# Scans a step behind their sigmoids, low parts behind the scans, and mapped weights kept in SBUF for the first chunk

## The chip, the cores and the metric

The kernel runs on one core of one Trainium2 chip. The metric is the device time of one execution in microseconds.

## What is computed

A two-layer trunk over 2048 tokens of 1024 channels, in f32:

```python
# layer 0: pooling mixer
u, z = split(rms_norm(x, a_norm) @ a_w_in)
pooled = trailing means of u over 2, 4, 8, 16 frames (4 channel groups) - u
x = x + ((pooled @ w_group per group) * a_scale * silu(z)) @ a_w_out
x = x + (p[0] @ ple_w[0]) * sigmoid(x @ ple_gate_w[0])
# keys and values once; layer 1: stick-breaking attention, 16 heads of 64
k, v = split(rms_norm(x, kv_norm) @ w_kv); q, z = split(rms_norm(x, b_norm) @ b_w_in)
A[t,s] = beta[t,s] * prod_{s<j<t} (1 - beta[t,j]),  beta = sigmoid(q.k / 8), s < t
x = x + ((A @ v) * silu(z)) @ b_w_out
x = x + (p[1] @ ple_w[1]) * sigmoid(x @ ple_gate_w[1])
```

Pooling is linear in time and `w_group` acts on channels, so the kernel multiplies `w_in`'s u half by `w_group` once ("mapped weights", `wf`) and pools the mapped product.

## The kernel before

**Tiles.** Tokens go through in four chunks of 512. Channels lie on partitions, and a matmul is 128 x 128 weights by 128 x 512 activations. Each f32 operand is split into a high part, rounded to f32r by ScalarE, and a low part (the difference); a product is three matmuls, high by high, high by low, low by high (L223, L227, L230 in `product`, L244, L246, L249 in `product2`, L490 for q, k and v, where activations are the weights side).

**Weights.** `plan` lists all weight units in the order of use. `pump` loads them ahead into buffers of the tag `wpair`, at most `UNITS` = 9 at a time: a unit that is used again is split once, written to DRAM (L152) and read back ready from there (L145, `wpair<-once` or `wpair<-wf`). `take` hands units out, `give_back` frees them. Raw loads (`wraw`, L148), x tiles and the columns of `w_in` (`uraw`, L262) share four buffers, tag `io`.

**First chunk.** For group g, `fold` makes the mapped weights on PE: 48 matmuls of 256 columns (L279) from the group weights and from four blocks of `w_in`, cast and split by `fold_load` (L266 `uh`, L267 `ul`). ScalarE and VectorE scale the result and split it (L285, L286) into `wf`, a buffer of the tag `at`, of which there are three; SP writes it to DRAM (L289), and `pump` reads it back (L145) as the next units. `pump` stops at the mapped units of `plan` (`src` None) until `fold` has written them. `mixer` runs the groups 3, 2, 1, 0: the fold, the z product (L223 to L230 with weights `wz_a`), then the u product with the mapped weights. `prep(0)` splits x (L119, L120), squares it (L350) and sums the squares with one-column matmuls (L355).

**Attention.** A slot is one head, one chunk of queries and one chunk of keys; it has four steps, of 128 queries each. Step n does, in program order: `turn` of step n-5 (four transposes, L736, of the products into a `psa` bank; ScalarE's high part `at`, L739; VectorE's low part, L740), `front` of step n (two matmuls for the logits, L721 and L722; the sigmoid of the negated logits, L724; a running product along keys, L726, called the scan below), a share of the dense products of the next chunk (`fill`), `gather` of step n-7 (L748 with the high part, L749 with the low), and another share. `psa`, `psl`, `pso`, `psd` have two PSUM banks each; `pp`, which holds sigmoids and running products, has nine buffers.

**Order.** A scheduler puts the instructions of each engine in order at build time by priorities and its own model; program order holds only where a dependency or `keep_in_program_order` demands it, which binds an instruction behind the one traced just before it on its engine. `state["pin"]` does that to the first matmul of each k pair of `product`, in the slots of the last chunk. The dense products of chunk c+1 run in the slots of chunk c, layer 1's output products in the slots of the last.

**z of layer 1.** In `gate_z` the first block of z is made before the norm is known; the norm is then broadcast (`bcast`, L297) at the 20th matmul of the next product, and the two kept tiles are multiplied by it.

Of the kernel before, what the change touches and what calls it, by code (L numbers as in the profile page):

```python
# [15 lines left out]
P = 128  # L16
# [20 lines left out]
def trunk_kernel(ctx, tc, x, p, a_norm, wu_t, wz_a, w_group, a_scale, a_w_out, kv_norm, w_kv,  # L37
# [158 lines left out]
    for s in range(NSUB):  # L196
        for g in (3, 2, 1, 0):
            if s == 0:
                plan_group(g)
            plan_block("za", wz_a, g, g_a, True)  # L200
            plan_block("wf", None, g)
        for b in range(4):
            plan_block("ao", a_w_out, b, order=PAIRS[::-1])
        for b in range(4):
            plan_block("ag", gate_a, b)
            plan_block("al", ple_a, b, order=PAIRS[:1])
        if s + 1 == NSUB:
# [5 lines left out]
        plan_kvq(1)  # L213
    for c in range(NSUB):
        plan_post()

# [53 lines left out]
    def fold(g):  # L270
        parts = maps.pop(g)
        (wg, _), = take(1)
        for kts in PAIRS:
            ps = dense().rearrange("q (e n) -> q e n", e=2)
            for e, kt in enumerate(kts):
                ks = slice(kt % 4 * P, kt % 4 * P + P)
                for c in range(2):
                    for l, r in ((0, 0), (1, 0), (0, 1)):
                        T.matmul(ps[:, e], parts[c, kt // 4][l][:, ks], wg[:, r, c],  # L279
                                 start=(c == 0 and l == r), stop=(c == 1 and r == 1))  # L280
# [8 lines left out]
            nc.sync.dma_start(out=d, in_=f(pr))  # L289
        give_back()  # L290
# [43 lines left out]
    def prep(s):  # L334
        ck = chunk[s]
        ck["x"] = []
        for o in range(KT):
            if s:
                xin = io("xin")
                nc.sync.dma_start(out=xin, in_=x[o * P : (o + 1) * P, s * W5 : (s + 1) * W5])  # L340
            else:
                xin = first_x[o]
            pr = pair("xp")
            split(pr, xin, G if s else V)
            ck["x"].append(pr)
            if s:
                gather_squares(ck, "acc1", o, xin)
            else:
                sq = tmp("sq")
                A.activation(out=sq, in_=xin, func=AF.Square)  # L350
                if o == 0:
                    sums = turned()
                for j in range(4):
                    tc.keep_in_program_order(
                        T.matmul(sums[:, 0, j : j + 1], sq[:, j * P : (j + 1) * P], ones,  # L355
                                 start=(o + j == 0), stop=(o == KT - 1 and j == 3)))
# [224 lines left out]
    def gate_z(s):  # L581
# [133 lines left out]
    def front(st, j):  # L715
# [6 lines left out]
        T.matmul(ps[:, :w], qb[:, qs], kk[:, :w], start=False, stop=True)  # L722
        pp = ppt("pp")
        A.activation(out=pp[:, r0:], in_=ps[:, :w], func=AF.Sigmoid, scale=-1.0)  # L724
        least = floor[:, r0:][:, ::-1] if st["diag"] else floor[:, 0:1].to_broadcast([P, w])
        V.tensor_tensor_scan(out=pp[:, r0:][:, ::-1], data0=pp[:, r0:][:, ::-1], data1=least,  # L726
                             initial=1.0 if st["diag"] else st["carry"][j], op0=ALU.mult, op1=ALU.max)
        st["carry"][j] = pp[:, r0 : r0 + 1]
        st["a"].append((pp, r0))

    def turn(st, kt):
        j0 = kt if st["diag"] else 0
# [4 lines left out]
        at = att("at")  # L737
        cs = slice(j0 * P, W5)
        A.copy(out=at[:, 0, cs], in_=pt[:, cs])  # L739
        V.tensor_tensor(out=at[:, 1, cs], in0=pt[:, cs], in1=f(at[:, 0, cs]), op=ALU.subtract)  # L740
        st["at"][kt] = at

    def gather(st, kt):
        cs = slice((kt if st["diag"] else 0) * P, W5)
# [53 lines left out]
        return (parts * 24.0) / (64 * (c + 1) - (5 if c < NSUB - 1 else 0))  # L798

    nc.scalar.dma_start(out=g_a, in_=a_norm)  # L800
    fold_load(3)
    pump()
    load_first()
    wq["by"] = nc.sync
    for dst, v in ((g_s, a_scale), (g_b, b_norm), (g_kv, kv_norm), (gs[:, 0:1], k_norm), (gs[:, 1:2], b_q_norm)):
        nc.scalar.dma_start(out=dst, in_=v)
    V.scalar_tensor_tensor(out=gqk, in0=gs[:, 1:2], scalar=HD ** -0.5, in1=gs[:, 0:1],
                           op0=ALU.mult, op1=ALU.mult)
    wq["cap"] = UNITS
    for _ in fold(3):  # L810
        pass
    for _ in prep(0):
# [11 lines left out]
    def fill(share):  # L824
        nonlocal owed, count
        owed += share
        while owed >= 1.0:
# [3 lines left out]
            if count % 36 == 0 and kept:  # L831
                keep(*kept.pop(0))

    for n in range(4 * len(slots) + LAG_G):
        i, j = divmod(n, 4)
        x_ = rate(i)
        i2, j2 = divmod(n - LAG_T, 4)
        if 0 <= i2 < len(slots):
            turn(active[i2], j2)
        if i < len(slots):  # L840
            state["pin"] = slots[i][0] == NSUB - 1
            if j == 0 and i + 1 < len(slots):
                begin(i + 1)
            if j == 3 and i + 1 < len(slots):
                begin_v(i + 1)
            front(active[i], j)
        fill(x_ / 2)
        i3, j3 = divmod(n - LAG_G, 4)
        if 0 <= i3 < len(slots):
            gather(active[i3], j3)  # L850
            if j3 == 3:
                active.pop(i3)
        fill(x_ / 2)
# [69 lines left out]
```

## Time and profile before

| | us |
|---|---|
| median of 3 runs | 2830.56 |
| lowest, highest | 2822.56, 2832.28 |
| the profiled execution | 2831.42 |
| its span, first to last instruction | 2829.6 |
| PE busy in it | 2731.6 |
| DVE (VectorE) busy | 1846.1 |
| ACT (ScalarE) busy | 1272.0 |
| POOL (GpSimd) busy | 878.4 |

PE is TensorE's matmuls, PEld its weight loads, which overlap them; SPq is SP's DMA queue. A row of a group has the source line, the engine, output and inputs by their names in the program, the count, the busy time and the mean of one in ns, then the idle time of the engine just before such instructions and what ended most of it. A row of a stretch has from:to, its length, the busy time and instructions of the five, PE's granted clock (1.00 is full), the DMA engines' share and GB/s. A wait's row has the total, the times and the longest.

### The profile page before, as it was taken

What the parts mean: (1) busy time and instruction counts of PE and PEld (TensorE: products, weight loads), DVE (VectorE), ACT (ScalarE), POOL (GpSimd) and SP (SyncE); (2) the same over time, 40 slices, a digit from 0 to 9 for tenths busy, and PEclk for the clock granted to TensorE, in tenths of its full rate; (3) what the DMA queues carried; (4) which work ended last, traced back from release to release, by engine and by line L of the source; (5) the groups of instructions that cost most, each with busy time, mean ns of one, the idle gap of its engine ahead of it and who ended that gap; (6) DMA issues with size and microseconds to landing.
All of it is one profiled execution on the core that took longest, in us unless ns stands there. A gap on an engine that the chain in (4) does not pass through costs nothing.

```text
span 2829.6 us, 38580 instructions
## 1 busy us (share of the span) xinstructions
PE 2731.6 (97%) x13400; PEld 2257.3 (80%) x13400; DVE 1846.1 (65%) x2369; ACT 1272.0 (45%) x2496; POOL 878.4 (31%) x699
## 2 busy tenths in 40 slices
PE   7999989998999999999999999999999999999999
PEld 6778867877878888878888788777877888888767
DVE  4646445757244677755678888756667777778763
ACT  4335444345444345544444555544445444444441
POOL 1255533556533244443222434211211201112002
PEclk8999999999999999999999999999999999999999
DMA  6756899978887855667885447567567767667535
GB/s 231 260 170 235 313 336 367 353 217 275 300 296 272 270 166 175 201 201 249 273 289 179 134 136 229 164 214 241 170 221 236 247 203 260 196 221 243 163 120 186
DMA packets 302799, 651.81 MB, mean 230 GB/s; under 512 B 51462, under 2 KB 84230, under 8 KB 302604
## 3 DMA queue, kind: packets, MB, share of 16 engines
q1 hardware_dynamic: 301020, 648.02, 69.3%
q8 instruction: 106, 1.74, 0.3%
q10 hardware_dynamic: 1584, 1.33, 0.1%
q14 instruction: 89, 0.73, 0.1%
HBM read 479.82 MB, written 161.02 MB: 226 GB/s over the span
## 4 chain that ended last, share of the span: by engine, by line
PE 68%; DVE 4%; DMA 4%; issue 1%; ACT 1%; POOL 1%; SPq 0%; ACTq 0%; DVEq 0%; POOLq 0%
PE psd L490 14%; PE psd L223 9%; PE psd L227 9%; PE psd L230 9%; PE psa L736 7%; PE pso L749 4%; PE pso L748 4%; PE psl L722 4%; PE psl L721 4%; DVE pp L726 2%; PE psd L244 2%; PE psd L249 2%; PE psd L246 2%; DMA wpair<-once 1%; DMA kk<-kd 1%
## 5 line engine op out<-in xcount | busy, mean ns | idle before, releaser
L726 DVE TENSOR_TENSOR_SCAN pp<-pp,floor 128x512 f32<-128x512 f32 (+3 forms) x640 | 769.7, 1220 | 166.5 <-ACT pp L724 164.5
L490 PE MATMUL psd<-wpair,x 128*128 128x512 f32 x2304 | 593.2, 398 | 11.7 <-DMA wpair<-once 3.0
L740 DVE TENSOR_TENSOR at<-psa,at 128x512 fp32r<-128x512 f32 (+3 forms) x640 | 379.1, 599 | 251.4 <-ACT at L739 249.8
L739 ACT CAST at<-psa 128x512 fp32r<-128x512 f32 (+3 forms) x640 | 331.3, 522 | 412.9 <-PE psa L736 388.7
L490 PEld LDWEIGHTS psd<-wpair,x 128*128 128x128 f32 x2304 | 427.5, 190 | 100.5 <-ACT qs L530 4.7
L724 ACT ACTIVATE pp<-psl 128x512 f32<-128x512 f32 (+3 forms) x640 | 330.1, 535 | 262.7 <-PE psl L722 159.8
L736 PE MATMUL psa<-ident,pp 128*128 128x128 f32 x2176 | 349.3, 276 | 29.1 <-DVE at L740 21.9
L736 PEld LDWEIGHTS psa<-ident,pp 128*128 128x128 f32 x2176 | 272.9, 142 | 107.7 <-DVE at L740 37.2
L749 PE MATMUL pso<-at,vv 128*128 128x512 f32 (+3 forms) x640 | 271.7, 425 | 0.4 <-DVE at L740 0.2
L721 PE MATMUL psl<-kk,qa 128*128 128x512 f32 (+3 forms) x640 | 243.8, 382 | 11.3 <-DMA kk<-kd 6.5
L748 PE MATMUL pso<-at,vv 128*128 128x512 f32 (+3 forms) x640 | 236.0, 371 | 3.1 <-ACT at L739 3.1
L223 PE MATMUL psd<-x,wpair 128*128 128x512 f32 x592 | 233.4, 394 | 2.5 <-ACT sg L466 2.5
L722 PE MATMUL psl<-kk,qb 128*128 128x512 f32 (+3 forms) x640 | 235.1, 368 | 0.0
L227 PE MATMUL psd<-x,wpair 128*128 128x512 f32 x592 | 232.6, 393 | 0.0
L230 PE MATMUL psd<-x,wpair 128*128 128x512 f32 x592 | 232.1, 392 | 0.0
L223 PE MATMUL psd<-xp,wpair 128*128 128x512 f32 x512 | 206.2, 403 | 8.8 <-DMA wpair<-wf 5.6
L227 PE MATMUL psd<-xp,wpair 128*128 128x512 f32 x512 | 205.3, 401 | 0.0
L230 PE MATMUL psd<-xp,wpair 128*128 128x512 f32 x512 | 204.3, 400 | 0.0
L133 POOL TENSOR_TENSOR wpair<-wraw,wpair 128x512 fp32r<-128x512 f32 x98 | 146.4, 1500 | 116.9 <-ACT wpair L131 116.7
L721 PEld LDWEIGHTS psl<-kk,qa 128*128 128x128 f32 x640 | 122.1, 191 | 36.0 <-ACT pp L724 12.9
L459 POOL TENSOR_TENSOR xj<-x 128x512 f32<-128x512 f32 x64 | 105.4, 1650 | 141.9 <-DVE sg L470 137.7
L764 POOL TENSOR_TENSOR os<-os,zt 128x512 f32<-128x512 f32 x32 | 46.3, 1446 | 306.3 <-ACT os L763 247.6
(162 smaller groups left out, 4696.8 us busy)
## 6 DMA issues: line engine op xcount, KB each, us to landing
wpair<-once SPq DMA_DIRECT2D x384, 512.0 KB
once<-wpair SPq DMA_DIRECT2D x80, 512.0 KB
kk<-kd SPq DMA_DIRECT2D x320, 128.0 KB
vv<-vd SPq DMA_DIRECT2D x160, 256.0 KB
wpair<-wf SPq DMA_DIRECT2D x64, 512.0 KB
once<-kp SPq DMA_DIRECT2D x36, 512.0 KB
wraw<-in_a_w_out_dram SPq DMA_DIRECT2D x64, 256.0 KB
wraw<-in_gate_a_dram SPq DMA_DIRECT2D x64, 256.0 KB
```

Of the source, the lines that this page charges most:

```text
L223: ins = T.matmul(ps, hi, acts[kt][:, 0], start=(i == 0), stop=False)
L227: T.matmul(ps, hi, acts[kt][:, 1], start=False, stop=False)
L230: T.matmul(ps, lo, acts[kt][:, 0], start=False, stop=(i == n))
L490: T.matmul(ps, ck["x2"][kt][:, xh, tk], u[:, wh, 0], start=(kt == 0 and xh == wh), stop=(kt == KT - 1 and wh == 1))
L721: T.matmul(ps[:, :w], qa[:, qs], kk[:, :w], start=True, stop=False)
L722: T.matmul(ps[:, :w], qb[:, qs], kk[:, :w], start=False, stop=True)
L726: V.tensor_tensor_scan(out=pp[:, r0:][:, ::-1], data0=pp[:, r0:][:, ::-1], data1=least, initial=1.0 if st["diag"] else st["carry"][j], op0 ...
L736: T.transpose(pt[:, j * P : (j + 1) * P], pp[:, r0 + kt * P : r0 + (kt + 1) * P], ident)
L739: A.copy(out=at[:, 0, cs], in_=pt[:, cs])
L740: V.tensor_tensor(out=at[:, 1, cs], in0=pt[:, cs], in1=f(at[:, 0, cs]), op=ALU.subtract)
L748: T.matmul(po[:, cs], vv[:, kt, :], at[:, 0, cs], start=(st["diag"] and kt == 0), stop=False)
L749: T.matmul(po[:, cs], vv[:, kt, :], at[:, 1, cs], start=False, stop=(st["last"] and kt == 3))
```

## The change

1. `fold` writes the mapped weights straight into buffers of the tag `wpair` and appends them to the units held; `pump` doesn't read them back in the first chunk. The write to DRAM stays, for the later chunks.
2. At the start the group weights are loaded before the columns of `w_in`, and the queue of units opens fully right behind x. The squares of chunk 0 and their matmuls come behind all splits.
3. In `gate_z` the broadcast goes to the 9th matmul, and the two kept tiles are multiplied at the 21st of this product and of the next.
4. `front` returns its scan, which is issued a step later, behind the next step's sigmoid; `turn` returns its low part, which is issued behind that scan. Both are bound behind what was traced before them on VectorE.
5. `state["pin"]` holds in the slots of the last two chunks.

```diff
     def pump():
...
-            if src is None and key not in once:
+            if src is None and (key not in once or wq["out"] < first_chunk):
                 return
...
-            pr = att("wf").rearrange("q l (e n) -> q l e n", e=2)
+            pr = pool.tile([P, 2, 2, WB], F32R, tag="wpair", name="wpair", bufs=UNITS)
...
+            assert plan[wq["out"]][0] == ("wf", g, kts) and wq["out"] - wq["back"] < UNITS
+            held.append((pr, kts))
+            wq["out"] += 1
             d = once["wf", g, kts] = scratch(f"wf{g}_{kts[0]}", [P, 2, 2, WB])
             nc.sync.dma_start(out=d, in_=f(pr))
...
-                sq = tmp("sq")
-                A.activation(out=sq, in_=xin, func=AF.Square)
-                if o == 0:
+                if o == KT - 1:
                     sums = turned()
-                for j in range(4):
...
+                    for i in range(KT):
+                        sq = tmp("sq")
+                        A.activation(out=sq, in_=first_x[i], func=AF.Square)
...
-                    if first and o == 2 and i == 20:
-                        ck["rb2"] = rb = bcast(ck["r2"], "y")
-                        for e, zr in enumerate(first):
-                            V.tensor_tensor(out=zr, in0=zr, in1=rb, op=ALU.mult)
-                            put(e, zr)
+                    if first and o == 2 and i == 9:
+                        ck["rb2"] = bcast(ck["r2"], "y")
+                    if first and o in (2, 3) and i == 21:
+                        zr = first[o - 2]
+                        V.tensor_tensor(out=zr, in0=zr, in1=ck["rb2"], op=ALU.mult)
+                        put(o - 2, zr)
...
     nc.scalar.dma_start(out=g_a, in_=a_norm)
+    pump()
     fold_load(3)
-    pump()
     load_first()
     wq["by"] = nc.sync
+    wq["cap"] = UNITS
+    pump()
...
+    scan = None
     for n in range(4 * len(slots) + LAG_G):
...
-            turn(active[i2], j2)
+        low = turn(active[i2], j2) if 0 <= i2 < len(slots) else None
+        due, scan = scan, None
         if i < len(slots):
-            state["pin"] = slots[i][0] == NSUB - 1
+            state["pin"] = slots[i][0] >= NSUB - 2
...
-            front(active[i], j)
+            scan = front(active[i], j)
+        if due:
+            due()
+        if low:
+            low()
         fill(x_ / 2)
```

Lines in the changed kernel: L225, L229, L232 for L223, L227, L230; L268 and L269 for L266 and L267; L281 for L279; L287 and L288 for L285 and L286; L294 for L289; L358 and L361 for L350 and L355; L302 for L297; L728, L729, L731 for L721, L722, L724; L736 for the scan L726; L748, L751, L754 for the turn's L736, L739, L740; L761 and L762 for L748 and L749.

What moves, at three places. First SP's queue in the first chunk, at the mapped weights of group 2 (`wf2_0` is their first unit in DRAM, `once` a split z unit's copy). Before:

```order
L289 DMA wf2_0_804<-wf_799 128x1024
L289 DMA wf2_2_824<-wf_819 128x1024
L289 DMA wf2_4_844<-wf_839 128x1024
L145 DMA wpair_866<-wf2_0_804 128x1024
L145 DMA wpair_868<-wf2_2_824 128x1024
L289 DMA wf2_6_864<-wf_859 128x1024
L145 DMA wpair_870<-wf2_4_844 128x1024
L145 DMA wpair_872<-wf2_6_864 128x1024
L148 DMA wraw_962<-in_wz_a_dram 128x512
L152 DMA once16_923<-wpair_916 128x1024
L262 DMA uraw_975<-in_wu_t_dram 128x512
```

And now:

```order
L294 DMA wf2_0_796<-wpair_791 128x1024
L294 DMA wf2_2_816<-wpair_811 128x1024
L148 DMA wraw_946<-in_wz_a_dram 128x512
L294 DMA wf2_4_836<-wpair_831 128x1024
L294 DMA wf2_6_856<-wpair_851 128x1024
L152 DMA once16_907<-wpair_900 128x1024
L264 DMA uraw_959<-in_wu_t_dram 128x512
```

The four reads are gone, and the next z load and the columns for the next map follow the writes.

Second VectorE in the slots of chunk 2 (a scan has `floor` among its inputs; a low part writes `at`; the rest belongs to dense products). Before:

```order
L726 SCALAR_TENSOR_TENSOR pp_16354<-pp_16354,floor_67 128x256
L726 SCALAR_TENSOR_TENSOR pp_16382<-pp_16382,floor_67 128x384
L740 TENSOR_TENSOR at_16316<-psa_16311,at_16316 128x512
L740 TENSOR_TENSOR at_16348<-psa_16343,at_16348 128x512
L726 SCALAR_TENSOR_TENSOR pp_16429<-pp_16429,floor_67 128x512
L469 TENSOR_TENSOR sg_16880<-psd_16882,sg_16880 128x512
L726 SCALAR_TENSOR_TENSOR pp_16455<-pp_16455,pp_16325,floor_67 128x512
```

And now:

```order
L736 SCALAR_TENSOR_TENSOR pp_16320<-pp_16320,floor_67 128x256
L120 TENSOR_TENSOR ple_16369<-pin_16367,ple_16369 128x512
L736 SCALAR_TENSOR_TENSOR pp_16348<-pp_16348,floor_67 128x384
L754 TENSOR_TENSOR at_16343<-psa_16338,at_16343 128x512
L133 TENSOR_TENSOR wpair_16539<-wraw_16540,wpair_16539 128x512
L754 TENSOR_TENSOR at_16388<-psa_16383,at_16388 128x512
L736 SCALAR_TENSOR_TENSOR pp_16395<-pp_16395,floor_67 128x512
L754 TENSOR_TENSOR at_16413<-psa_16408,at_16413 128x512
```

Scans and low parts stood in pairs, the scans further ahead; now they mostly alternate.

Third ScalarE at the start, ahead of the first z weights (`xp` the split of x, `sq` its squares, `uh` the high part of a block of `w_in`). Before:

```order
L350 ACTIVATE sq_536<-xin_353 128x512
L119 CAST xp_542<-xin_355 128x512
L350 ACTIVATE sq_545<-xin_355 128x512
L119 CAST xp_551<-xin_357 128x512
L119 CAST xp_560<-xin_359 128x512
L137 ACTIVATE wpair_367<-wraw_368,g_a_105 128x256 x2
```

And now:

```order
L119 CAST xp_509<-xin_359 128x512
L358 ACTIVATE sq_513<-xin_345 128x512
L358 ACTIVATE sq_519<-xin_347 128x512
L358 ACTIVATE sq_525<-xin_349 128x512
L358 ACTIVATE sq_531<-xin_351 128x512
L358 ACTIVATE sq_537<-xin_353 128x512
L358 ACTIVATE sq_543<-xin_355 128x512
L268 CAST uh_341<-uraw_327 128x512
L137 ACTIVATE wpair_361<-wraw_362,g_a_105 128x256 x2
```

The squares stand behind the casts, and the last block's cast, which stood ahead of all of this, stands right ahead of the z weights.

More of the change, by code (lines that the diff above doesn't have):

```diff
@@ L348, in prep @@
             else:
-                sq = tmp("sq")
-                A.activation(out=sq, in_=xin, func=AF.Square)
-                if o == 0:
+                if o == KT - 1:
                     sums = turned()
-                for j in range(4):
-                    tc.keep_in_program_order(
-                        T.matmul(sums[:, 0, j : j + 1], sq[:, j * P : (j + 1) * P], ones,
-                                 start=(o + j == 0), stop=(o == KT - 1 and j == 3)))
+                    for i in range(KT):
+                        sq = tmp("sq")
+                        A.activation(out=sq, in_=first_x[i], func=AF.Square)
+                        for j in range(4):
+                            tc.keep_in_program_order(
+                                T.matmul(sums[:, 0, j : j + 1], sq[:, j * P : (j + 1) * P], ones,
+                                         start=(i + j == 0), stop=(i == KT - 1 and j == 3)))
             yield
@@ L724, in front, with scan @@
         A.activation(out=pp[:, r0:], in_=ps[:, :w], func=AF.Sigmoid, scale=-1.0)
[L725 to L729, printed above, removed]
+        def scan():
+            least = floor[:, r0:][:, ::-1] if st["diag"] else floor[:, 0:1].to_broadcast([P, w])
+            tc.keep_in_program_order(
+                V.tensor_tensor_scan(out=pp[:, r0:][:, ::-1], data0=pp[:, r0:][:, ::-1], data1=least,
+                                     initial=1.0 if st["diag"] else st["carry"][j], op0=ALU.mult, op1=ALU.max))
+            st["carry"][j] = pp[:, r0 : r0 + 1]
+            st["a"].append((pp, r0))
+        return scan
     def turn(st, kt):
@@ L739, in turn @@
         A.copy(out=at[:, 0, cs], in_=pt[:, cs])
-        V.tensor_tensor(out=at[:, 1, cs], in0=pt[:, cs], in1=f(at[:, 0, cs]), op=ALU.subtract)
         st["at"][kt] = at
+        return lambda: tc.keep_in_program_order(
+            V.tensor_tensor(out=at[:, 1, cs], in0=pt[:, cs], in1=f(at[:, 0, cs]), op=ALU.subtract))
     def gather(st, kt):
```

4 lines of the change are left out of this document (2 added, 2 removed).

## The prediction

> **What bounds the kernel now.** I read the head of the page first, then the clock, the stretches of time, the waits of PE stretch by stretch, and last SP's queue and the order of the engines.
>
> ```profile
> span 2829.6 us, 38580 instructions
> PE 2731.6 (97%) x13400; PEld 2257.3 (80%) x13400; DVE 1846.1 (65%) x2369; ACT 1272.0 (45%) x2496; POOL 878.4 (31%) x699
> core 0: 2829.6 us, clock 0.984
> ```
>
> PE is the bound: it is idle for 2829.6 - 2731.6 = 98.0 us, and the clock that it was not granted is 1.6% of the span, 45 us, part of that while idle (the whole run took 2831.4 us). The change leaves PE's matmuls as they are, in number and shape; so all that it can win lies in those two sums, and the question is where they lie. Three places matter. The first is the first chunk, columns PE, PEld, DVE, ACT, POOL, then granted clock, DMA share and GB/s:
>
> ```profile
> 79.00:86.00 7.00, 5.70 (x14) 4.48 (x15) 3.73 (x7) 2.44 (x7) 0.87 (x1) 0.51 0.87 295
> 113.00:120.00 7.00, 5.97 (x14) 4.74 (x15) 3.67 (x6) 2.25 (x6) 2.09 (x2) 0.52 0.88 304
> 147.00:151.00 4.00, 3.98 (x11) 3.15 (x12) 0.84 (x1) 1.25 (x3) 4.00 (x4) 0.57 0.82 298
> ```
>
> PE's waits around these three stretches, one answer each:
>
> ```profile
> PE psd L223 <- DMA wpair<-wf: 3.3, 1, 3.3
> ...
> PE psd L223 <- DVE wpair L138: 3.2, 1, 3.2
> ...
> PE psd L223 <- DMA wpair<-wf: 2.3, 1, 2.3
> ```
>
> Each time PE has finished a group's z product and waits for the mapped weights; the clock halves right after. (The second is put down to VectorE, but that instruction works on other units; a read of mapped weights was in flight there too.) SP's queue at the first of them shows why:
>
> ```profile
> 72.08 1.63 SPq L289 DMA_DIRECT2D wf<-wf  x3
> 74.77 1.66 SPq L145 DMA_DIRECT2D wpair<-wf  x2
> 77.10 0.32 SPq L289 DMA_DIRECT2D wf<-wf  x1
> 78.12 5.19 SPq L145 DMA_DIRECT2D wpair<-wf  x2
> 83.38 0.42 SPq L148 DMA_DIRECT2D wraw<-in_wz_a_dram  x1
> ```
>
> And PE's next matmul there:
>
> ```profile
> 80.30 0.77 PE L223 MATMUL psd<-xp,wpair 128*128 128x512 f32 x1 [3.30 <-DMA wpair<-wf]
> ```
>
> The weights lie in SBUF by 72 us, go out to DRAM, and come back behind that write; PE wants them 3.30 us before 80.30, at 77.0 us.
>
> The second place is attention in chunks 2 and 3, where PE stands idle in a few short stretches; the last row but two is the steady rest:
>
> ```profile
> 1540.00:1700.00 160.00, 155.80 (x794) 129.24 (x793) 136.24 (x156) 84.14 (x170) 64.84 (x47) 1.00 0.48 147
> 1770.00:1804.00 34.00, 27.27 (x150) 21.73 (x149) 27.94 (x36) 18.24 (x38) 3.06 (x2) 0.95 0.47 143
> 1854.00:1869.00 15.00, 10.53 (x48) 7.70 (x48) 14.01 (x17) 9.26 (x18) 0.56 (x2) 0.89 1.00 341
> 1917.00:1934.00 17.00, 12.42 (x66) 9.96 (x66) 12.61 (x20) 9.30 (x18) 1.11 (x1) 0.90 1.00 324
> 2057.00:2078.00 21.00, 15.24 (x75) 11.12 (x75) 17.73 (x22) 12.66 (x27) 2.59 (x2) 0.92 0.80 274
> 2129.00:2147.00 18.00, 14.94 (x85) 11.15 (x84) 17.76 (x24) 12.11 (x25) 0.30 (x1) 1.00 0.99 328
> 2147.00:2600.00 453.00, 452.74 (x2321) 376.60 (x2320) 340.29 (x409) 208.06 (x402) 61.55 (x40) 1.00 0.69 222
> 2676.00:2732.00 56.00, 49.00 (x243) 36.36 (x244) 49.22 (x58) 30.98 (x63) 2.54 (x2) 0.94 0.35 113
> 2732.00:2752.00 20.00, 18.32 (x91) 14.01 (x90) 7.66 (x11) 5.96 (x12) 0.45 (x1) 1.00 0.25 80
> ```
>
> Where PE loses, VectorE is busy 74 to 99% of the time; from 2147 to 2600 us, where attention steps and dense products alternate evenly, PE loses 0.3 us in 453.
>
> **The first chunk (mapped weights).** Removed: 16 reads of 512 KB, the waits for them, and SP's standing behind them. The waits are 3.3 + 3.2 + 2.3 = 8.8 us. The half clock after them: 5.70 us of PE work at 0.51 would take 2.9 us at full clock, so 2.8 go; likewise 5.97 x 0.48 = 2.9 and 3.98 x 0.43 = 1.7. Together 8.8 + 7.4 = 16.2 us.
>
> [...]
>
> What is late next: the fourth z load of the next group and the loads for its map, which SP issues from 83.38 us on, behind the reads. With the reads gone SP gets there about 78 us, some 5.5 us earlier, which is as much as PE gains; so they should keep their distance. If they don't, PE waits for the next map instead, and of 5.4 us a group little is left (a rival below). The added wait, a wpair buffer for the map's result, is for a unit used nine units before, thus the same quarter of the group before, whose product PE has finished; the write to DRAM stays, but nothing near reads it. Range of this term: -17 to -4.
>
> **The start.** The first map may begin as soon as its group weights and two of four column blocks are there; before, PE stood until these rows:
>
> ```profile
> 13.26 0.34 ACTq L806 DMA_DIRECT2D gs<-in_b_q_norm_dram  x1
> 14.31 0.58 PE L279 MATMUL psd<-wpair,uh 128*128 128x256 f32 x1 [14.31 <-ACT wpair L131]
> 14.91 0.41 PE L279 MATMUL psd<-wpair,uh 128*128 128x256 f32 x1
> 15.12 0.41 PE L279 MATMUL psd<-wpair,ul 128*128 128x256 f32 x1
> 21.45 3.31 ACT L137 ACTIVATE wpair<-wraw,g_a 128x256 fp32r<-128x256 f32 x8
> 21.65 7.60 PE L355 MATMUL pst<-ones,sq 128*128 128x1 f32 x48
> 33.52 3.41 PE L355 MATMUL pst<-ones,sq 128*128 128x1 f32 x16
> ```
>
> The clock over the last of it:
>
> ```profile
> 24.50:41.60 17.10, 17.10 (x60) 15.10 (x61) 4.43 (x11) 4.47 (x12) 1.23 (x2) 0.50 0.94 345
> ```
>
> PE can start some 6 us earlier, but gains nothing: ScalarE still passes eight casts and six squares, and now the fourth block's cast too (the group weights' cast has left that stretch, so the count is the same), before the z weights at about 21.5 us. The last third of the map, 18 matmuls, waits for that cast; then come the 64 one-column matmuls, whose 7.60 + 3.41 = 11.0 us are in one piece now. Before, PE had the map behind it at 21.65. So PE is later by 18 matmuls, at the 0.21 us between the starts at 14.91 and 15.12 3.8 us, less the idle before 14.31 that no longer counts and less whatever the clock recovers sooner from dense work after 37 us. I take +1.5 us, between -3 (the clock back a window earlier) and +5.
>
> **Attention.** One scan and one low part a step, and no instruction less:
>
> ```profile
> L726 DVE TENSOR_TENSOR_SCAN pp<-pp,floor 128x512 f32<-128x512 f32 (+3 forms) x640 | 769.7, 1220 | 166.5 <-ACT pp L724 164.5
> L736 PE MATMUL psa<-ident,pp 128*128 128x128 f32 x2176 | 349.3, 276 | 29.1 <-DVE at L740 21.9
> L740 DVE TENSOR_TENSOR at<-psa,at 128x512 fp32r<-128x512 f32 (+3 forms) x640 | 379.1, 599 | 251.4 <-ACT at L739 249.8
> ```
>
> VectorE needs 1.22 + 0.60 = 1.82 us a step. PE's own part of a step is shorter: in 1770 to 1804 it did 150 matmuls in 27.27 us busy, 0.18 us each, and a step has eight, 1.45 us. So a bunch of steps with no dense matmul between them is VectorE's, and PE waits. Before, the idle time of the six stretches up to 2147 is 4.2 + 6.7 + 4.5 + 4.6 + 5.8 + 3.1 = 28.9 us, and the clock missing in four of them 0.05 x 34 + 0.11 x 15 + 0.10 x 17 + 0.08 x 21 = 6.7: 35.6 us.
>
> Counted in PE's order, runs of four or more turns without a dense matmul between them: before, from chunk 1's end until products grow short, 17, 4, 8, 8 and 12, which are the last five of the six stretches in order; after, 5, 4, 4, 4, 4, 8, 4, 12 and 4. As many turns, 49 each, but the run of 17 and one of 8 are broken up (the wider pin). At the end, where products have run out, 37 before and 36 after. Two long runs and the run of 4 remain at 3.1 + 4.6 + 1.7 + 4.5 + 1.7 = 15.6; the six new short ones I put at 1.5 each, 9 us, between nothing (the buffers carry four steps) and 3; the thin loss of the first stretch at 2. That is 26.6, 9 us less. Against it stands VectorE's order: before, in 172 of chunk 2's 192 steps a scan stood 7 or 8 steps ahead of the last low part; after, in 145 of them 5, which is the lag that the loop itself gives. Two scans, 2.4 us, are no longer done when a run begins. With half of that at two runs in the middle and half at the end, 3 us. So -6, between -16 and +12. The scan that no longer stands waiting for its sigmoid (164.5 us) is VectorE's gain, and PE sees it only in the runs, where it is in the sum. The bcast moved from the 20th to the 9th matmul lands at the same place in PE's order, 6.8 us of matmuls after its norm, and so costs nothing; the two products behind it are spread over work that VectorE has room for.
>
> **Sum.** -16.2 + 1.5 - 6 = -20.7 against the profiled execution's 2831.4 us, which is 0.9 above the median of 2830.6: **2810 us**.
>
> **The rivals.**
> *The loads take the reads' place.* PE then waits for the next map's columns at each group, as long as before less a microsecond or so, and the clock falls again. For it: SP's queue is in order and those loads are its next rows. Against: they depended on nothing else at 83.38 us. The sum is -3 + 1.5 - 4, about 2825 us.
> *VectorE in lockstep: slower.* Scans and low parts are bound to what stands ahead of them, five steps ahead at most, in all 13 runs; each run pays the 2.4 us of the two scans that were ahead before, nothing of the breaking up is won: -16.2 + 1.5 + 13 x 2.4 = +16.5, 2847 us. It decides from 1.8 us a run on. For it: PE waited on low parts already (21.9 us); against: 1.82 us a step is the same sum of work in either order. [...]
> *The runs are cured.* The low part, no longer behind two or three scans, frees its bank in time, and the short runs cost nothing: -16.2 + 1.5 - 20 = 2796 us. Steady 2147 to 2600 speaks for it, the unchanged run of 12 against.
>
> **How the numbers follow.** Forecast 0.60, loads 0.16, lockstep 0.12, cured 0.12. A measurement of this kernel can tell about 0.3%, 8.5 us, from no change: faster is below 2822, slower above 2839. Of the forecast 0.58 lies below 2822; the cured runs do whole; of the loads 0.03. Faster 0.73. Same takes 0.02 + 0.13 + 0.03 = 0.18, slower the lockstep's 0.09. The range leaves out lockstep and the lower part of the cured case: 2796 to 2828.
>
> **What would show it.** Right: no wait of L225 on mapped weights and a granted clock over 0.95 between 60 and 150 us; the first chunk's end 15 us earlier; the first matmul near 8 us, yet the zs product no earlier; fewer idle stretches between 1700 and 2100. Wrong: waits of PE on L269's columns in the first chunk (loads), or idle before the transposes over 45 us in all (lockstep).

## The result, and the profile after

| | before | after |
|---|---|---|
| median, us (13 runs each) | 2828.37 | 2833.48 |
| lowest, highest | 2821.71, 2832.28 | 2828.38, 2837.83 |
| ratio, 95% interval | | 1.0021 [1.0012, 1.0031] |

The changed kernel is 5 us slower where 20 us less was forecast; by the bound of 0.3% that is no change, and it lies above the range. The head of its page:

```profile
span 2831.7 us, 38727 instructions
PE 2729.6 (96%) x13400; PEld 2250.0 (79%) x13400; DVE 1832.6 (65%) x2369; ACT 1275.0 (45%) x2496; POOL 873.3 (31%) x699
core 0: 2831.7 us, clock 0.986
```

PE's busy time (2731.6 us before, 2729.6 now) and clock (0.984, 0.986) hardly moved, so the same sum of losses must lie elsewhere. The first chunk, columns as before:

```profile
60.00:150.00 90.00, 90.00 (x466) 77.46 (x465) 66.32 (x116) 36.63 (x74) 32.02 (x33) 1.00 0.57 202
```

The matmuls of the first chunk's products wait for no read of mapped weights:

```profile
L225 PE MATMUL psd<-xp,wpair 128*128 128x512 f32 x512 | 203.5, 398 | 0.5 <-DMA wpair<-once 0.5
```

The kernel before, over the same 90 us:

```profile
60.00:150.00 90.00, 81.04 (x390) 68.23 (x391) 56.14 (x108) 34.16 (x69) 25.20 (x27) 0.91 0.73 254
```

That part did what was foreseen: no idle time, full clock. To follow the gain I take the time at which the same piece of PE's work is reached, counting the matmuls of the trace (13400 in each):

| matmul | before, us | after, us | difference |
|---|---|---|---|
| 500th | 127.9 | 115.9 | -12.0 |
| 1000th | 240.3 | 224.2 | -16.1 |
| 2000th | 476.3 | 460.8 | -15.5 |
| 6500th (chunk 2's slots begin) | 1421.2 | 1406.8 | -14.4 |
| 10000th (110 us into chunk 3's) | 2139.2 | 2132.4 | -6.8 |
| 12000th | 2530.3 | 2525.1 | -5.2 |
| 13000th (chunk 3's slots end) | 2734.0 | 2734.3 | +0.3 |

16 us are won in the first 1000 matmuls and given back in the attention of chunks 2 and 3. The groups of attention, of after:

```profile
L736 DVE TENSOR_TENSOR_SCAN pp<-pp,floor 128x512 f32<-128x512 f32 (+3 forms) x640 | 779.0, 1219 | 5.2 <-ACT pp L731 4.6
L754 DVE TENSOR_TENSOR at<-psa,at 128x512 fp32r<-128x512 f32 (+3 forms) x640 | 378.7, 595 | 312.9 <-ACT at L751 311.1
L748 PE MATMUL psa<-ident,pp 128*128 128x128 f32 x2176 | 357.4, 276 | 45.0 <-DVE at L754 23.7 <-DVE pp L736 13.8 <-DVE hl L120 4.6
```

The scan no longer waits for its sigmoid (166.5 us, now 5.2), but VectorE then waits ahead of low parts (251.4, now 312.9), and PE's transposes wait 45.0 us for 29.1. 13.8 of it is new: they wait for the scan itself. One such place, VectorE and then PE of after (start, duration, instruction, idle time before it and who ended it):

```profile
1434.09 1.21 DVE L736 TENSOR_TENSOR_SCAN pp<-pp,floor 128x512 f32<-128x512 f32 x1
1435.22 0.66 DVE L754 TENSOR_TENSOR at<-psa,at 128x512 fp32r<-128x512 f32 x1
1438.11 0.69 DVE L767 TENSOR_TENSOR os<-pso,os 64x512 f32<-64x512 f32 x1 [2.23 <-ACT os L766]
1438.84 1.28 DVE L736 TENSOR_TENSOR_SCAN pp<-pp,floor 128x512 f32<-128x512 f32 x1
```
```profile
1437.53 0.49 PE L761 MATMUL pso<-at,vv 128*128 128x512 f32 x1
1441.45 0.88 PE L748 MATMUL psa<-ident,pp 128*128 128x128 f32 x3 [3.43 <-DVE hl L120]
```

And ScalarE there:

```profile
1434.88 0.63 ACT L731 ACTIVATE pp<-psl 128x512 f32<-128x512 f32 x1
1435.76 0.60 ACT L731 ACTIVATE pp<-psl 128x512 f32<-128x512 f32 x1 [0.25 <-PE psl L729]
```

Sigmoids ended at 1435.51 and 1436.36, and VectorE was idle 2.23 us up to 1438.11, yet no scan ran between 1435.3 and 1438.84: L767, the sum of the two halves of a head's output, stood ahead of it and waited for ScalarE's copy. So the binding does hold scans that could run. PE's 3.43 us, though, ended by its row with L120 and not with a scan: L120 reads keys that stand transposed in one of the two `psa` banks, and the next transposes need a bank. The clock was halved (0.51 granted) from 1440.8 to 1447.7. That is a reading of one place. Whether the binding is the cause, and of the whole loss, the experiments had to show.

### The profile page after: what moved, and what is told of

It reads as the page before. It is cut to its first block, busy times and chain, and to the rows that moved or that the text cites. A ratio compares the mean times of both kernels' runs of the same rounds, so it can differ in the third digit from the quotient of the medians.

```text
span 2831.7 us, 38727 instructions
## 1 busy us (share of the span) xinstructions
PE 2729.6 (96%) x13400; PEld 2250.0 (79%) x13400; DVE 1832.6 (65%) x2369; ACT 1275.0 (45%) x2496; POOL 873.3 (31%) x699
## 4 chain that ended last, share of the span: by engine, by line
PE 78%; DMA 8%; DVE 7%; ACT 2%; issue 2%; POOL 1%; SPq 1%; ACTq 0%; DVEq 0%; POOLq 0%
PE psd L496 15%; PE psd L225 11%; PE psd L229 11%; PE psd L232 11%; PE psa L748 7%; PE pso L762 4%; PE psl L729 4%; PE psl L728 3%; PE pso L761 3%; DVE pp L736 3%; PE psd L251 2%; PE psd L248 2%; PE psd L246 2%; DMA wpair<-once 2%; DVE at L754 1%
## 5 line engine op out<-in xcount | busy, mean ns | idle before, releaser
L736 DVE TENSOR_TENSOR_SCAN pp<-pp,floor 128x512 f32<-128x512 f32 (+3 forms) x640 | 779.0, 1219 | 5.2 <-ACT pp L731 4.6
L496 PE MATMUL psd<-wpair,x 128*128 128x512 f32 x2304 | 582.9, 395 | 10.0 <-ACT wpair L137 3.9
L754 DVE TENSOR_TENSOR at<-psa,at 128x512 fp32r<-128x512 f32 (+3 forms) x640 | 378.7, 595 | 312.9 <-ACT at L751 311.1
L751 ACT CAST at<-psa 128x512 fp32r<-128x512 f32 (+3 forms) x640 | 330.9, 523 | 378.3 <-PE psa L748 358.7
L731 ACT ACTIVATE pp<-psl 128x512 f32<-128x512 f32 (+3 forms) x640 | 333.4, 535 | 305.8 <-PE psl L729 194.8
L748 PE MATMUL psa<-ident,pp 128*128 128x128 f32 x2176 | 357.4, 276 | 45.0 <-DVE at L754 23.7
L748 PEld LDWEIGHTS psa<-ident,pp 128*128 128x128 f32 x2176 | 272.9, 141 | 132.0 <-DVE at L754 38.7
L762 PE MATMUL pso<-at,vv 128*128 128x512 f32 (+3 forms) x640 | 275.1, 430 | 0.6 <-DVE at L754 0.6
L728 PE MATMUL psl<-kk,qa 128*128 128x512 f32 (+3 forms) x640 | 244.3, 382 | 13.2 <-DMA kk<-kd 9.8
L761 PE MATMUL pso<-at,vv 128*128 128x512 f32 (+3 forms) x640 | 238.7, 374 | 7.6 <-DMA once<-kp 5.4
L729 PE MATMUL psl<-kk,qb 128*128 128x512 f32 (+3 forms) x640 | 236.0, 370 | 0.0
L225 PE MATMUL psd<-x,wpair 128*128 128x512 f32 x592 | 233.5, 394 | 0.0
L232 PE MATMUL psd<-x,wpair 128*128 128x512 f32 x592 | 232.5, 393 | 0.0
L229 PE MATMUL psd<-x,wpair 128*128 128x512 f32 x592 | 232.5, 393 | 0.0
L225 PE MATMUL psd<-xp,wpair 128*128 128x512 f32 x512 | 203.5, 398 | 0.5 <-DMA wpair<-once 0.5
L229 PE MATMUL psd<-xp,wpair 128*128 128x512 f32 x512 | 201.7, 394 | 0.0
L232 PE MATMUL psd<-xp,wpair 128*128 128x512 f32 x512 | 201.2, 394 | 0.0
L133 POOL TENSOR_TENSOR wpair<-wraw,wpair 128x512 fp32r<-128x512 f32 x98 | 139.0, 1423 | 153.6 <-ACT wpair L131 152.5
L728 PEld LDWEIGHTS psl<-kk,qa 128*128 128x128 f32 x640 | 122.8, 192 | 40.8 <-ACT pp L731 11.2
L761 PEld LDWEIGHTS pso<-at,vv 128*128 128x128 f32 x640 | 122.0, 191 | 27.7 <-ACT at L751 11.0
```

What stands on the lines that cost most here:

```text
L225: ins = T.matmul(ps, hi, acts[kt][:, 0], start=(i == 0), stop=False)
L229: T.matmul(ps, hi, acts[kt][:, 1], start=False, stop=False)
L232: T.matmul(ps, lo, acts[kt][:, 0], start=False, stop=(i == n))
L496: T.matmul(ps, ck["x2"][kt][:, xh, tk], u[:, wh, 0], start=(kt == 0 and xh == wh), stop=(kt == KT - 1 and wh == 1))
L728: T.matmul(ps[:, :w], qa[:, qs], kk[:, :w], start=True, stop=False)
L748: T.transpose(pt[:, j * P : (j + 1) * P], pp[:, r0 + kt * P : r0 + (kt + 1) * P], ident)
```

## The experiments

**Theory:** the binding of the scan behind everything that was traced before it on VectorE holds ready scans back, and this costs what the first chunk wins. **Rivals:** the wider pin does it; the delay by a step does it (bound or not); the low part's binding does it; the first chunk's gain is itself undone later by its loads; and, as the expectations below have it (theory C), any change gives the scheduler another order of attention, which costs by chance.

**1. Parts alone and left out.** Five kernels, each with some of the parts. All of the change but part 4 (`front` scans at once, `turn` makes its low part at once, neither bound):

```diff
-            scan = front(active[i], j)
+            front(active[i], j)
...
-        if due:
-            due()
-        if low:
-            low()
```

> The whole change without its part 4: scans and low parts are issued as before, in the scheduler's free order; the first chunk's weights, the start, the broadcast and the wider pin stay. Theory V (VectorE's bound order costs what the first chunk saves): the first chunk keeps its 16 us, attention loses nothing: 2812 us, ratio to before 0.994. Theory P (the wider pin costs it): no better than the whole change, 2833 us, 1.002. Theory C (a scheduler that is given other input puts attention in another order, and any change of it costs by chance): anywhere, 2812 to 2840.

2815.7 us, 0.9951 [0.9935, 0.9968]. All but the wider pin:

```diff
-            state["pin"] = slots[i][0] >= NSUB - 2
+            state["pin"] = slots[i][0] == NSUB - 1
```

> The whole change without its part 5: only the last chunk's slots bind the first matmul of each k pair. Theory V: the loss stays, 2830 to 2836 us, 1.001. Theory P: the loss goes, 2812 to 2816 us, 0.995. Theory C: anywhere between.

2821.1 us, 0.9977 [0.9965, 0.9989]. Parts 1 and 2 alone (first chunk and start; of the diff the hunks of `pump`, `fold`, `prep` and the start):

> The kernel before with parts 1 and 2 alone: mapped weights kept in SBUF and the new start. All theories but C: the first chunk's 16 us reach the end, since attention is as before: 2812 us, 0.994. Theory C: the scheduler's order of attention changes with it and takes part of it back: 2815 to 2830.

2819.8 us, 0.9964 [0.9952, 0.9977]. Part 4 alone (scan and low part a step later, bound; the hunks of `front`, `turn` and the loop but for `state["pin"]`):

> The kernel before with part 4 alone: scans a step later, low parts behind them, both bound. Theory V: slower by what the whole change lost in attention, 16 to 20 us: 2844 to 2848 us, 1.006. Theory P: no different from before, 2828 us, 1.000.

2832.9 us, 1.0016 [1.0005, 1.0028]; its profiled execution, span 2819.9 us, was the shortest of its runs. Part 5 alone, the wider pin, against the kernel before:

```diff
-            state["pin"] = slots[i][0] == NSUB - 1
+            state["pin"] = slots[i][0] >= NSUB - 2
```

> The kernel before with part 5 alone, the wider pin. The first four runs left 12 us that the pin costs beside part 4, and 4 us that it won without it. Theory V+P (the pin is harmless until VectorE's bound order makes PE wait, since pinned products cannot be moved ahead into the wait): 2822 to 2828 us, 0.998. Theory P (the pin costs by itself): 2836 us or more, 1.003.

2822.6 us, 0.9988 [0.9975, 1.0001].

What follows: the first chunk keeps a gain, no part alone was measured to cost more than 0.2%, and yet leaving out either part 4 or part 5 makes the whole faster than before. Three of these expectations missed. Part 4 alone was to cost 16 to 20 us and costs 0.16%, so the theory fell as it stood; leaving out the pin was to change nothing or to end the whole loss, and did neither; the first chunk and start gave 2819.8 us for 2812. The last two lie where only theory C had them. So two parts must cost together what neither does alone. The direct test is parts 4 and 5 without the rest:

> The kernel before with the scan and low part a step later, both bound, and the wider pin, without anything of the first chunk, the start or z of layer 1. Alone the delayed and bound scan was +4 us (1.0016) and the pin -3 us (0.9988). Theory, the two together cost what neither does alone, because pinned products can't be put into the gap that a held scan leaves: 1.004 to 1.006, about 2840 us. Rival, the parts add up: 1.0004, about 2829 us.

2840.2 us, 1.0057 [1.0037, 1.0076]. Adding the parts gives 1.0016 x 0.9988 = 1.0004: the theory of a joint cost holds, the sum of parts falls. With that the eight cases are complete (part 3 goes with parts 1 and 2 in the right column, but for its first row; "scan bound" stands for the whole of part 4):

| | without parts 1 and 2 | with them | their worth |
|---|---|---|---|
| scan free, narrow pin | 1 | 0.9964 | -0.36% |
| scan free, wide pin | 0.9988 | 0.9951 | -0.37% |
| scan bound, narrow pin | 1.0016 | 0.9977 | -0.39% |
| scan bound, wide pin | 1.0057 | 1.0021 | -0.36% |

The first chunk and start are worth 0.36 to 0.39%, some 10.5 us, in every row, and part 3 adds nothing that shows. Part 4 costs 0.13 to 0.16% under the narrow pin and 0.69 to 0.70% under the wide one. The figures repeat pair by pair, which speaks against theory C's chance.

**2. Delay or binding, scan or low part.** The changed kernel with both delayed as there, neither bound:

```diff
-            tc.keep_in_program_order(
-                V.tensor_tensor_scan(...))
+            V.tensor_tensor_scan(...)
...
-        return lambda: tc.keep_in_program_order(
-            V.tensor_tensor(...))
+        return lambda: V.tensor_tensor(...)
```

> The whole change, the scan still a step later and the low part behind it in the text, but neither bound in order. Theory B (binding costs: a bound scan stands behind whatever was traced before it): 2814 to 2818 us, 0.996, as without part 4. Theory L (coming a step later costs): 2833 us, 1.002.

2817.5 us, 0.9964 [0.9953, 0.9976]. Only the first of these two edits, so the scan is free and the low part bound:

> The whole change with only the low part bound, the scan free. Theory B, the scan's binding costs (transposes waited 13.8 us for scans, which before they did not): 2816 us, 0.996. Theory B, the low part's binding costs: 2833 us, 1.002.

2814.0 us, 0.9959 [0.9943, 0.9975]. Only the second, so the scan is bound and the low part free:

> The whole change with only the scan bound, the low part free. The scan's binding costs: 2831 to 2834 us, 1.002. The low part's binding costs: 2816 us, 0.996.

2831.0 us, 1.0009 [0.9995, 1.0024], which can't be told from the whole change. So it is the binding of the scan; the delay by a step and the low part's binding cost nothing that shows. The scan's binding alone is then worth 1.0021 against 0.9959 to 0.9964, some 0.6%, 16 to 18 us. The same groups, with the scan free:

```profile
L735 DVE TENSOR_TENSOR_SCAN pp<-pp,floor 128x512 f32<-128x512 f32 (+3 forms) x640 | 772.9, 1218 | 182.2 <-ACT pp L731 180.0
L753 DVE TENSOR_TENSOR at<-psa,at 128x512 fp32r<-128x512 f32 (+3 forms) x640 | 379.2, 600 | 252.3 <-ACT at L750 250.6
L747 PE MATMUL psa<-ident,pp 128*128 128x128 f32 x2176 | 348.0, 275 | 27.0 <-DVE at L753 20.8 <-DVE hl L120 3.7 <-DVE hl L559 2.1
```

The scans wait for their sigmoids again, 182.2 us, PE's wait for the scan is gone, and the kernel is 0.6% faster: waiting in front of a scan was harmless. The same place as above, VectorE, scan free:

```profile
1432.45 2.46 DVE L735 TENSOR_TENSOR_SCAN pp<-pp,floor 128x512 f32<-128x512 f32 x2
1434.82 0.67 DVE L753 TENSOR_TENSOR at<-psa,at 128x512 fp32r<-128x512 f32 x1
1435.52 0.69 DVE L766 TENSOR_TENSOR os<-pso,os 64x512 f32<-64x512 f32 x1
1436.24 1.28 DVE L735 TENSOR_TENSOR_SCAN pp<-pp,floor 128x512 f32<-128x512 f32 x1
```

The head's sum comes without a wait, and two scans went ahead of it. Yet PE gains nothing there: from the 6500th to the 7000th matmul, which take in this place, the changed kernel needs 108.0 us and this one 107.6. The place shows what the binding does, not where it costs; that is in 3. One row warns against reading too much from one wait: with the scan bound and the low part free, PE's idle time before the transposes is 28.4 us, less than before, while the time is as long as with both bound:

```profile
L748 PE MATMUL psa<-ident,pp 128*128 128x128 f32 x2176 | 359.4, 276 | 28.4 <-DVE at L753 19.3 <-DVE pp L736 4.4 <-DVE hl L559 2.6
```

Its loss is in other waits (8.8 us on the high part, 8.2 on sigmoids). Only the time over a piece of work tells:

| kernel | scan | pin in chunk 2 | 6500th to 10000th matmul, us | 10000th to 13000th |
|---|---|---|---|---|
| before | free | no | 718.0 | 594.8 |
| first chunk and start alone | free | no | 718.3 | 596.7 |
| part 1 alone | free | no | 722.0 | 596.0 |
| pin alone | free | yes | 714.0 | 595.4 |
| all but part 4 | free | yes | 715.2 | 597.2 |
| only the low part bound | free | yes | 714.9 | 596.3 |
| only the low part bound, old start | free | yes | 715.2 | 596.2 |
| neither bound | free | yes | 715.5 | 604.4 |
| part 4 alone | bound | no | 712.3 | 599.0 |
| all but the pin | bound | no | 715.5 | 601.2 |
| after | bound | yes | 725.6 | 601.9 |
| only the scan bound | bound | yes | 725.3 | 600.1 |
| parts 4 and 5 | bound | yes | 725.4 | 602.2 |
| scans free in chunk 2 (experiment 3) | free, then bound | yes | 718.8 | 599.6 |

In the first of these stretches a bound scan costs 10 us where the products are pinned (725.3 to 725.6 for 714.0 to 715.5) and nothing where they aren't (712.3 and 715.5 for 718.0 to 722.0). In chunk 3, where the pin held in every kernel, it costs 4.8 us in the mean, 600.9 for 596.1, whatever holds in chunk 2 (the last row is in neither mean). One row breaks the pattern and is left out, 604.4 with neither bound; with it the free mean is 597.1. That trace, of the slowest of the kernel's 12 runs, has a wait of 3.06 us for keys at 2214 us and 6.8 us at half clock with it. Whether that is chance is open.

**3. Where.** The scans of chunk 2's slots are freed, those of the other chunks stay bound:

```diff
-            tc.keep_in_program_order(
-                V.tensor_tensor_scan(...))
+            ins = V.tensor_tensor_scan(...)
+            if st["c"] != 2:
+                tc.keep_in_program_order(ins)
```

> The changed kernel, but the running products of chunk 2's slots (the slots of its queries, about 1410 to 2030 us) are not bound to program order; those of the other chunks still are. In the changed kernel 12.6 us of the first chunk's gain are given back between 1407 and 1520 us and about 8 us between 2530 and 2630 us. Theory, the binding of the scans costs what it costs where other VectorE work is traced ahead of a scan, in several places: the give-back in chunk 2 goes, the one in chunk 3 stays, about 2821 us, and the wait of PE's transposes on the scan itself falls from 13.8 us to under half. Rival, the cost sits only where chunk 3's products are pinned: about 2833 us as with all bound. Second rival, it sits only in chunk 2: about 2814 us, as with all scans free.

2822.9 us, 0.9985 [0.9973, 0.9997]: between the two rivals, as the theory has it. The pieces of PE's work show where (us from one matmul to another; a range is over the kernels of the table above with that scan and pin, the mixed one apart):

| scan | pin in chunk 2 | 6500th to 7000th | 7000th to 9000th | 9000th to 10000th | 12200th to 12600th |
|---|---|---|---|---|---|
| free | no | 98.5 to 98.8 | 413.7 to 416.9 | 204.8 to 206.3 | 77.7 to 77.8 |
| free | yes | 107.1 to 109.5 | 406.5 to 408.6 | 199.3 to 199.5 | 77.7 to 77.8 |
| bound | no | 98.8 to 99.0 | 410.7 to 411.2 | 202.7 to 205.3 | 82.2 to 84.8 |
| bound | yes | 105.3 to 108.0 | 416.0 to 418.3 | 201.3 to 201.6 | 83.1 to 85.7 |
| free in chunk 2, then bound | yes | 110.0 | 408.4 | 200.4 | 82.2 |

The wider pin costs 9 us at the start of chunk 2, bound or free, and wins 7 us from the 7000th matmul on and 6 more from the 9000th. With bound scans the 7 are not won (416.0 to 418.3). Free the scans of chunk 2, and they are won again (408.4), while the last column, in chunk 3, stays dear (82.2). So one premise of the expectation is wrong: the give-back between 1407 and 1520 us is the pin's, and it stays. Before, after, with the scans of chunk 2 free, and with all free:

```profile
1407.00:1520.00 113.00, 113.00 (x573) 94.58 (x573) 82.53 (x106) 46.72 (x93) 27.56 (x26) 1.00 0.80 258
1407.00:1520.00 113.00, 105.38 (x525) 85.99 (x525) 81.83 (x103) 49.72 (x102) 23.86 (x21) 0.97 0.67 211
1407.00:1520.00 113.00, 105.61 (x516) 84.64 (x515) 85.15 (x105) 48.45 (x99) 20.92 (x19) 0.95 0.65 206
1407.00:1520.00 113.00, 103.94 (x523) 84.39 (x522) 83.68 (x101) 48.31 (x98) 25.14 (x21) 0.98 0.68 213
```

In the last column of the table lies a place where bound and free do part. VectorE, then PE, of after:

```profile
2574.16 1.26 DVE L475 TENSOR_TENSOR sg<-psd,sg 128x512 f32<-128x512 f32 x2
2575.34 1.28 DVE L476 TENSOR_TENSOR sg<-sg,xj 128x512 f32<-128x512 f32 x2
2576.54 2.30 DVE L736 TENSOR_TENSOR_SCAN pp<-pp,floor 128x512 f32<-128x512 f32 x1
2578.76 0.66 DVE L754 TENSOR_TENSOR at<-psa,at 128x512 fp32r<-128x512 f32 x1
2579.35 2.61 DVE L736 TENSOR_TENSOR_SCAN pp<-pp,floor 128x512 f32<-128x512 f32 x2
2581.88 0.66 DVE L754 TENSOR_TENSOR at<-psa,at 128x512 fp32r<-128x512 f32 x1
```
```profile
2579.48 0.66 PE L748 MATMUL psa<-ident,pp 128*128 128x128 f32 x4 [2.15 <-DVE at L754]
2582.59 0.69 PE L748 MATMUL psa<-ident,pp 128*128 128x128 f32 x2 [1.98 <-DVE at L754]
```

And ScalarE, which makes the high parts:

```profile
2575.81 0.58 ACT L751 CAST at<-psa 128x512 fp32r<-128x512 f32 x1
2576.45 0.61 ACT L751 CAST at<-psa 128x512 fp32r<-128x512 f32 x1
```

The high parts were ready at 2576.39 and 2577.06, but their low parts ran at 2578.76 and 2581.88, behind scans, the first of which stood behind four dense operations and took 2.30 us beside one of GpSimd. PE waited 2.15 and 1.98 us, and the clock was halved (0.50 granted) from 2580.9 to 2587.7; with free scans PE waits nowhere in this piece. Chunk 2's slots, and 100 us of chunk 3's, of after:

```profile
1407.00:2030.00 623.00, 595.58 (x3007) 488.62 (x3007) 462.86 (x568) 301.93 (x600) 169.03 (x134) 0.99 0.61 193
2530.00:2630.00 100.00, 94.97 (x474) 78.18 (x474) 71.60 (x84) 41.91 (x82) 15.61 (x10) 0.97 0.69 220
```

With the scans of chunk 2 free:

```profile
1407.00:2030.00 623.00, 603.93 (x3038) 497.96 (x3037) 474.88 (x572) 307.23 (x604) 171.03 (x133) 0.98 0.61 194
2530.00:2630.00 100.00, 95.96 (x490) 79.19 (x489) 74.60 (x89) 43.94 (x87) 15.68 (x10) 1.00 0.74 228
```

With all scans free:

```profile
1407.00:2030.00 623.00, 604.42 (x3051) 499.66 (x3050) 471.99 (x569) 308.35 (x604) 174.20 (x135) 0.98 0.61 193
2530.00:2630.00 100.00, 100.00 (x514) 83.28 (x513) 77.81 (x91) 46.80 (x89) 16.79 (x10) 1.00 0.72 226
```

PE's idle time in chunk 2 is 27.4 us bound, 19.1 with that chunk free, 18.6 with all free; in chunk 3's 100 us it is 5.0, 4.0 and none. The loss of the binding goes only where the binding goes. Another part of the expectation missed: the wait on the scan fell from 13.8 to 10.1 us, not under half.

**4. The start.** Only part 1, the start as before:

> The kernel before with only the mapped weights written straight into the first chunk's units; the start is as before. The same with the new start was 2819.8 us (0.9964). Theory from the sum on record, the start costs 1.5 us: 2818 us. Rival, the start wins by its earlier first matmul: 2823 us or more.

2814.7 us, 0.9964 [0.9949, 0.9978], the same ratio as with the new start. And the changed kernel with the scan free and without part 2:

> The changed kernel with the scan free (2814.0 us, 0.9959), and with the old start: squares among the splits, w_in's columns ahead of the group weights. If the start is worth nothing it stays at 2814; by the sum on record it gains 1.5 us, 2812.5; if the earlier first matmul is worth its 6 us it is 2819 or more.

2809.9 us, 0.9953 [0.9935, 0.9970], beside 0.9959 with the new start: the runs can't part them. The traces can. The 500th matmul comes at 111.0 us with part 1 alone and at 115.9 in the changed kernel. Its clock at the start:

```profile
17.50:27.70 10.20, 6.10 (x25) 5.72 (x25) 6.42 (x14) 8.58 (x20) 0.00 (x0) 0.50 0.40 141
31.10:41.40 10.30, 10.30 (x42) 9.53 (x42) 0.00 (x0) 0.16 (x1) 1.23 (x2) 0.50 0.75 293
```

And with part 1 alone, its only stretch at half clock there:

```profile
27.40:34.20 6.80, 6.80 (x23) 5.83 (x24) 2.15 (x6) 2.50 (x7) 1.28 (x1) 0.50 1.02 388
```

Half of 6.10 + 10.30 is 8.2 us lost, half of 6.80 is 3.4: 4.8 us, which is the difference of 4.9. So in the trace the new start costs 4.8 us, near the upper end foreseen. Over all kernels with part 1 the 500th matmul comes at 112.5 to 116.8 us with the new start and at 111.0 and 111.4 with the old. In the timed runs it is not shown: without part 2 and with free scans the kernel has the lowest median here, but its ratio, 0.9953, is no lower than the 0.9951 of all but part 4.

## Why the prediction was wrong

**First chunk, -16.2: right in mechanism, somewhat large.** No wait on mapped weights in the three groups, the clock 1.00, and no wait for the next map's columns, so the rival of the loads falls. The sum with the start should have been -14.7; the four pairs of kernels give -10.5 us in time. The traced pair shows -16.1, but the profiled execution of before had 17.1 us at half clock in its start. The six traces with that start had from 6.8 to 17.1; with the pin alone it was this:

```profile
27.10:34.00 6.90, 6.90 (x24) 6.00 (x24) 1.56 (x4) 1.54 (x4) 0.00 (x0) 0.51 1.02 397
```

Half of 17.1 - 6.9 is 5 us that the one execution lost and the other didn't. Over the four traces without part 1 the 1000th matmul comes at 233 to 241 us, and before's 240.3 is near the late end. A sum against one execution carries such chance; how the 4 us between -14.7 and -10.5 divide over the two terms is open.

**Start, +1.5 within -3 to +5: mechanism right.** The first matmul came at 7.82 us, PE then stood for the fourth block's cast as said:

```profile
14.49 0.28 PE L281 MATMUL psd<-wpair,uh 128*128 128x256 f32 x1
21.60 0.79 PE L281 MATMUL psd<-wpair,uh 128*128 128x256 f32 x2 [6.83 <-ACT uh L268]
```

What was left out is that the early start opens an idle gap (6.83 us, the row above) and with it a second stretch at half clock (17.50 to 27.70 us, 0.50). The lower end of the term, -3 for "the clock back a window earlier", was an estimate that no run shows: the clock was full again at 41.4 us in after and at 41.6 in before, and the shortest stretches at half clock in before, such as 147.4 to 150.8, are 3.4 us long.

**Attention, -6 within -16 to +12: the failed step.** Parts 4 and 5 without the rest measure +16 us (1.0057). The prediction took the wider pin's shorter runs for -9 us and the scans' smaller lead for +3, as two terms to be added. The first is -3 us alone (0.9988): the pin wins 13 us in the middle and end of chunk 2, but costs 9 at its start. The second is the error, "Two scans, 2.4 us, are no longer done when a run begins": it priced the new order by the scans that are missing at a run's start, as if a bound scan ran whenever its input was there. (That lead did shrink by about two; by after's trace a scan stands 5 steps ahead in 111 of chunk 2's 192 steps and 6 in 77, not 5 in 145.) A bound scan also waits for whatever the instructions ahead of it wait for, and with the products pinned the two parts came to 15 us beyond the sum of each alone (1.0057 for 1.0004: 0.53%). So the terms weren't independent.

**The scans' wait of 166.5 us** was called "VectorE's gain". It was gone, and it was no gain: VectorE's wait before low parts grew from 251.4 to 312.9 us, and PE's before transposes from 29.1 to 45.0.

**The lockstep rival came nearest,** at a wrong price. Its sign, over 45 us before the transposes, was just reached (45.0), though the kernel with the low part free shows the same loss with 28.4. It was priced at 37 us more than the forecast, 2847 us, 2.4 us at each of 13 runs, with nothing won by the pin; part 4 cost 0.70% beside all but part 4, 20 us, and the loss lies in a few pieces of the work, not shown run by run. The chance of 0.12 was too low: the rival had scans and low parts bound to what stands ahead of them, but was priced by the lead that the scans lose, and not by the waits of what is traced ahead of them, such as L767's 2.23 us up to 1438.11 with a scan behind it.

**What stays open:** why the pin makes the binding dear. The pieces show where: with bound scans the pin's 7 us from the 7000th to the 9000th matmul are not won. They don't show by which wait: over that piece PE stands 19.8 us bound and 11.0 free, and the difference is spread over waits for low parts, keys and scans. PE's order differs between these kernels as well, in so many places that it could not be held fixed while VectorE's was changed. That pinned products can't be put into the gap which a late scan leaves was argued, and the joint cost agrees with it, but no run shows the mechanism by itself.

## What to carry to other kernels

Binding an instruction to program order binds it to the waits of everything traced ahead of it on its engine (here a scan stood behind a head's sum that waited 2.23 us), not just to the two or three instructions that one had in mind; ask of each what it may wait for. Idle time of an engine that is not the bound, in front of an instruction, can be slack and not loss: with 182 us of it the kernel was 0.6% faster than with 5. Two constraints on the order, on two engines, can each cost next to nothing and be dear together (1.0016 and 0.9988 apart, 1.0057 together), so time them together and apart before adding up. And a place that looks like the cause is one only if the other kernel does the same piece of work faster.

## What the runs showed of the hardware

**One-column matmuls didn't keep the clock up.** In the changed kernel the squares' sums run in one piece:

```profile
27.31 10.55 PE L361 MATMUL pst<-ones,sq 128*128 128x1 f32 x64
37.72 0.77 PE L232 MATMUL psd<-xp,wpair 128*128 128x512 f32 x1
```

PE is never idle there by the trace, and still the clock is half from 31.1 us on, 3.8 us after these begin, until 41.4, 3.7 us after dense matmuls return (the row 31.10:41.40 above: busy 10.30 of 10.30, clock 0.50). With part 1 alone they begin at 23.3 us and the clock falls at 27.4. In before they begin at 21.65 us and it falls at 24.5; in all 14 traces here it falls 2.5 to 5.3 us after they begin. In before the rest of them (3.41 us) came before the clock was back, and it stayed at half for 17.1 us. So 10.55 us of such matmuls without a gap did not hold the full clock, which was granted from 27.7 to 31.1 us.

**A scan beside GpSimd.** In the changed kernel 278 scans of 512 columns had no GpSimd operation beside them and took 1.27 us in the mean, 1.285 at most; 170 had one and took 1.58, up to 2.41. Before it was much the same (1.27 and 1.61), so this explains nothing of the result. Why a scan is longer beside GpSimd was not shown.
